# Four-bank token-major projections, branches ahead of retention, and an earlier start of the v product in a four-stage transformer on one core

## The chip, the cores and the metric

The program runs on one core of a Trainium2 chip. The time is what the device takes for one execution, in microseconds (us); runs of the same kernel are compared by their medians. All data lie in HBM at the start and the result is written back there. The core's engines are TensorE (PE in the rows, its weight loads PEld), VectorE (DVE), ScalarE (ACT), GpSimd (POOL) and SyncE (SP, which here only issues transfers).

## What is computed

The reference takes 512 tokens of width 1024 through these stages, all in float32:

- block 1: a norm, then two branches side by side, a gated delta rule in both directions and an attention with dilated windows, gated and added to the stream;
- a PEER layer: each token picks 16 of 16384 experts in each of 8 heads by two sets of 128 keys. An expert is one row of a table u and one of a table v: `y = sum over picked experts of weight * gelu(x . u_e) * v_e`;
- block 2, twice: a norm, then three branches of it, each with a gate of width 1024,

```
a = latent attention (MLA)      b = stick-breaking attention      c = retention
m = sigmoid(gate_a) * (a Wa) + sigmoid(gate_b) * (b Wb) + sigmoid(gate_c) * (c Wc)
h = h + m Wo
h = h + square(relu(norm(h) Wup)) Wdown
```

- the last row of the stream goes through a final norm.

## The kernel before

**Matmuls.** A float32 product is made of three matmuls on rounded halves: a number x is split into xh (rounded) and xl = x - xh, and W x becomes Wh xh + Wh xl + Wl xh. Weights come from HBM in tiles of 128x1024, 512 KB each, by SP's queue (`raw<-...`, method `pump`, line 632). ACT rounds such a tile to its high half and DVE subtracts to get the low half (both `whl<-raw` in the rows; `split`, `split_low`). Activations lie with features on partitions and 512 tokens along the columns, as eight tiles of 128x512 with a high and a low half (`s` in the rows). `unit` is the common product: one weight tile, 24 matmuls of 512 columns into one PSUM bank. The eight banks are two lists: `bmain` with two banks, for the products of the main path, and `bside` with six, for the side jobs (attention and so on).

**Order.** The program is written out instruction by instruction by the class `Prog`, in one order for each engine. The main path is a generator; after each piece of it a model of the clocks, kept while the program is built, decides whether a piece of a side job is put in between (`tick`), so that side work fills engines beside the main products. `wait` and `idle` let side work run on until a job is done. `BACKLOG`, `RAW` and `AHEAD` set how far side work and weights may run ahead. Each engine works its list in order; all helpers record through line 307, which is why nearly all rows have that line.

**Token-major projections.** Two of the branches need v with tokens on partitions. `tm_unit` (line 715) takes two weight tiles, which together hold 256 of 512 output columns for all 1024 inputs. It goes through four groups of 128 tokens, one after the other: 24 matmuls of 256 columns into one bank of `bmain`, then the bank is given to `tok_epi` (line 2046), which scales it on ACT into half a tile. Two calls, one for each half of the columns, make one projection: 192 matmuls, eight evictions. There are four projections: `stick` and `retain` in both layers.

**The peer stage** (`peer`). 384 tokens are computed densely: for each of 128 chunks of 128 experts, 24 matmuls of 384 columns against the tile of u (the u product), a gelu on ACT, and a write of the result to the DRAM tensor `ga` (the last 16 chunks are kept in SBUF). Side jobs route the tokens and write the experts' weights to the DRAM tensor `wd` (`wd<-big`, 24 writes on POOL's queue). The v product follows, with 128 chunks again, 24 matmuls each, and all eight banks accumulate through it (`acc`). For each chunk DVE multiplies gelu by the weights (`prep`, the `s<-s,big` rows), ACT and DVE split the product (`prep_low` makes the low half). `rows` reads the weights for eight chunks by three transfers of 512 KB (`big<-wd`). The first three of these, the first products and the job `rope_tables` (sines and cosines for block 2, a chain on DVE and ACT) are put in between u and v. The other 128 tokens are done by gathering single rows of u and v on POOL's queue (`picked`: `rows_u`, `rows_v`, products on DVE into `dbl`). The last two chunks (`last`) are kept back, so that the eight banks end one after the other, d = 0 to 7: for each, its last six matmuls and a transpose, then an addition on DVE, a scaled high half on ACT and a low half on DVE, which block 2 needs.

**Block 2** (`layer`). `ORDER` is: latents of branch a, 6 gate units, upward projections of a, projections of b (`stick`), 6 gate units, projections of c (`retain`), 12 gate units. A gate unit's result is written to the DRAM tensor `gd`. The side jobs of a, b and c run beside this. Then the main path waits for all three jobs, splits their 12 result tiles into halves (`hilo`), and makes the branches: for dp = 0 to 3 and each branch b two units of 12 matmuls, each multiplied by its sigmoid gate and summed. `Wo`, the norm and the MLP follow.

Of the kernel before, what the change touches and what calls it, by code (L numbers as in the profile page):

```python
# [26 lines left out]
TB = 16  # L27
# [48 lines left out]
BRANCHES = ((0, 0), (0, 2), (0, 4), (1, 0), (1, 2), (1, 4), (0, 6), (1, 6))  # L76
ORDER1 = ("da0", "k", "q", "da1", "da2", "v", "z", 16)
# [70 lines left out]
def layouts(x, norm_mix, w_in, dn_conv, dn_a_log, dn_dt_bias, dn_out_norm, rel_bias, w_branch_dn,  # L148
# [45 lines left out]
    for l in range(2):  # L194
# [21 lines left out]
        f[f"w_b{l}"] = np.stack([_fm_tiles(w_branch_2[l, b], 2) for b in range(3)], 1).reshape(12, 128, 1024)  # L216
# [94 lines left out]
class Prog:  # L311
# [403 lines left out]
    def tm_unit(self, xs, sels, epi):  # L715
        w0 = self.get()
        w1 = self.get(more=True)
        for n, sel in enumerate(sels):
            ps = self.bank(q=self.bmain)
            for i in range(8):  # L720
                hi, lo = (w0, w1)[i // 4]
                s = slice((i % 4) * 256, (i % 4) * 256 + 256)
                xh, xl = sel(xs[i][0]), sel(xs[i][1])
                m = xh.shape[1]
                self.mm(ps[:m, :256], xh, hi[:, s], start=i == 0, stop=False)
                self.mm(ps[:m, :256], xh, lo[:, s], start=False, stop=False)
                self.mm(ps[:m, :256], xl, hi[:, s], start=False, stop=i == 7)
                if i == 3:
                    self.flush()
            self.pend.append((lambda p, n=n, m=m: epi(n, p[:m, :256]), ps))  # L730
            yield
# [791 lines left out]
    def peer(self):  # L1523
# [43 lines left out]
        for c in range(128):  # L1567
            def epi(ps, c=c):
                t = self.slot(big=c < 128 - KEPT)
                self.act(t[:, :TD], ps[:, :TD], AF.Gelu_apprx_tanh)  # L1570
                if c < 128 - KEPT:
                    self.dma(ga[c], t[:, :TD], self.nc.sync)
                    self.put(t)
                else:
                    gts[c - 128 + KEPT] = t
            if c >= 128 - KEPT:
                self.room(4)
            yield from self.unit(self.get(), xs, epi)
        self.flush()
        self.wait(wt, rt_end)  # L1580
        self.put(ic)
        for a in self.xn:
            self.put(*a)
        self.BACKLOG, self.low_late = 4.0, True

        assert len(self.bmain) == 2 and len(self.bside) == 6
        acc = [self.bank(q=q) for q in (self.bmain, self.bside) for _ in range(len(q))]
        rt = self.add(self.rope_tables())
        self.close_big(1)
        bigs = [self.take_big(0), self.take_big(1)]  # L1590
        self.ring.extend(b[:, 8 * TD:8 * TD + 1024] for b in bigs)

        def rows(n, t0, k):
            w = bigs[n % 2][:, :8 * TD].rearrange("p (t i u) -> p t i u", i=8, u=TB)
# [27 lines left out]

        def step(d, c, v, h):
# [6 lines left out]
        for i in range(3):  # L1630
            rows(0, i * 8, 8)
        for c in range(6):
            fetch(c)
        for c in range(3):
            prep(c)
        prep_low(0)
        prep_low(1)
        last = range(126, 128)
        for c in range(last[0]):
            fetch(c + 6)  # L1640
            if c % 8 < 3 and c < 120:
                rows(c // 8 + 1, c % 8 * 8, 8)
# [960 lines left out]
```

## Time and profile before

| | |
|---|---|
| median of 3 runs | 3900.13 us (3897.69 to 3905.33) |
| the profiled execution | 3899.97 us, span 3898.0 us |
| TensorE busy | 3772.4 us, 97% of the span |
| mean granted TensorE clock | 0.986 |
| VectorE, ScalarE, GpSimd busy | 2541.1 (65%), 1536.9 (39%), 457.6 us (12%) |
| moved by transfers | 666.67 MB, mean 171 GB/s |

The span is the time from the first to the last instruction of one core; the execution's own time has some 2 us around it. Busy time of TensorE is the time in which a matmul is under way, at whatever clock; the granted clock is a share of full speed. A number in square brackets behind a row is the time for which the engine stood idle just before it, with what ended this.

### The profile page before, as it was taken

How to read it: one execution, taken by the hardware profiler on the slowest of the kernel's cores; microseconds unless marked ns; L12 is line 12 of the kernel's file. 1: busy time of each engine (PE TensorE's matmuls, PEld its weight loads, DVE VectorE, ACT ScalarE, POOL GpSimd, SP SyncE). 2: the span in 40 equal slices, each digit the busy share in tenths (PEclk: the TensorE clock that was granted, in tenths of full speed). 3: DMA queues.
4: the chain of work that ended last, by engine and by line, in shares of the span. 5: the costliest groups of instructions: out<-in, count | busy, mean ns of one | idle time of the engine just before them, and what ended most of it. 6: DMA issues, size and time to landing. Idle time of an engine off the chain costs nothing.

```text
span 3898.0 us, 56154 instructions
## 1 busy us (share of the span) xinstructions
PE 3772.4 (97%) x21866; PEld 3221.4 (83%) x21866; DVE 2541.1 (65%) x4608; ACT 1536.9 (39%) x2392; POOL 457.6 (12%) x524
## 2 busy tenths in 40 slices
PE   9999899999999979999989999999999999999998
PEld 6777777899889979999977876788888878678886
DVE  4565755789989868888766556654345656564334
ACT  3533334344545423333343453433233344343222
POOL 1010201011333433222200001000000001000000
PEclk9999999999999989999999999999999999999999
DMA  4232524376798989999933223432233223342222
GB/s 151 81 110 88 168 101 151 129 240 209 291 329 296 380 285 326 348 345 348 342 123 108 76 78 120 154 119 97 96 106 128 87 77 100 109 167 105 95 95 81
DMA packets 259114, 666.67 MB, mean 171 GB/s; under 512 B 27316, under 2 KB 105428, under 8 KB 255776
## 3 DMA queue, kind: packets, MB, share of 16 engines
q1 hardware_dynamic: 202752, 457.19, 34.3%
q0 software_dynamic: 55376, 204.80, 14.5%
q8 instruction: 172, 2.82, 0.3%
q10 hardware_dynamic: 720, 1.08, 0.1%
q14 instruction: 94, 0.77, 0.1%
HBM read 576.16 MB, written 81.57 MB: 169 GB/s over the span
## 4 chain that ended last, share of the span: by engine, by line
PE 58%; DVE 2%; ACT 2%; issue 1%; DMA 0%; DVEq 0%; ACTq 0%
PE bank L307 58%; DVE s L307 1%; ACT s L307 1%; DVE big L307 1%; ACT whl L307 0%; DMA big<-rope 0%; DVE whl L307 0%; ACT L555 0%; ACT big L307 0%; DVE mla_m L307 0%; DVE dbl L307 0%; ACT dbl L307 0%; DVE bank L307 0%; DVEq L2598 0%; DVEq L307 0%
## 5 line engine op out<-in xcount | busy, mean ns | idle before, releaser
L307 PE MATMUL bank<-s,whl 128*128 128x512 f32 (+1 forms) x15156 | 3276.1, 374 | 89.3 <-DVE whl L307 28.7
L307 PEld LDWEIGHTS bank<-s,whl 128*128 128x128 f32 x15156 | 2756.9, 189 | 502.4 <-issue 66.7
L307 DVE TENSOR_TENSOR whl<-raw,whl 128x1024 fp32r<-128x1024 f32 x651 | 795.1, 1222 | 484.1 <-ACT whl L307 481.0
L307 ACT ACTIVATE whl<-raw 128x1024 fp32r<-128x1024 f32 x651 | 683.1, 1055 | 685.3 <-PE bank L307 368.5
L307 DVE TENSOR_TENSOR big<-bank,big 128x512 f32<-128x512 f32 (+4 forms) x270 | 179.0, 666 | 300.0 <-PE bank L307 297.1
L307 DVE TENSOR_TENSOR s<-s,s 128x1024 f16<-128x1024 f16 (+9 forms) x498 | 295.1, 614 | 23.2 <-ACT s L307 13.2
L307 ACT ACTIVATE s<-bank 128x384 f32<-128x384 f32 (+6 forms) x263 | 122.0, 489 | 414.1 <-PE bank L307 406.6
L307 ACT ACTIVATE big<-big 128x512 f32<-128x512 f32 (+2 forms) x235 | 141.6, 615 | 323.4 <-DVE big L307 277.7
L307 ACT ACTIVATE big<-bank 128x512 f32<-128x512 f32 (+3 forms) x242 | 161.2, 712 | 254.5 <-PE bank L307 157.5
L307 ACT ACTIVATE s<-s 128x384 fp32r<-128x384 f32 (+7 forms) x321 | 162.6, 526 | 155.2 <-DVE s L307 151.1
L307 PE MATMUL bank<-s,s 128*128 128x128 f16 (+10 forms) x2102 | 209.2, 260 | 4.6 <-DVE s L307 4.6
L1701 POOL DMA_INDIRECT dbl<-rows_u,s x128 | 172.1, 1345 | 321.8 <-DVE dbl L307 135.3
L307 DVE TENSOR_TENSOR s<-s,big 128x384 f32<-128x384 f32 (+5 forms) x279 | 135.1, 488 | 47.1 <-DMA big<-wd 20.3
L582 POOL DMA_DIRECT2D s<-dbl x16 | 7.9, 500 | 1319.6 <-PE bank L307 1319.6
L307 DVE SCALAR_TENSOR_TENSOR dbl<-dbl,dbl 128x1024 f32<-128x1024 f32 x128 | 154.3, 1217 | 10.0 <-DMA dbl<-rows_u,s 10.0
L307 PEld LDWEIGHTS bank<-s,s 32*32 32x32 f32 (+5 forms) x1334 | 104.4, 146 | 37.0 <-issue 26.2
L1701 POOL DMA_INDIRECT dbl<-rows_v,s x94 | 103.6, 1102 | 258.9 <-DVE dbl L307 252.4
L307 ACT ACTIVATE s<-big 128x512 fp32r<-128x512 f32 (+2 forms) x136 | 90.6, 677 | 106.7 <-DVE big L307 104.7
L307 PE MATMUL bank<-s,big 32*32 32x32 f32 (+6 forms) x960 | 121.2, 283 | 1.7 <-ACT big L307 1.3
L307 PE MATMUL bank<-whl,s 128*128 128x256 f32 (+1 forms) x816 | 111.7, 297 | 9.3 <-ACT s L307 6.0
L307 DVE SCALAR_TENSOR_TENSOR dbl<-dbl,s,dbl 128x1024 f32<-128x1024 f32 x93 | 118.8, 1278 | 0.0
L307 DVE SCALAR_TENSOR_TENSOR big<-bank,big 128x512 f32<-128x512 f32 x74 | 51.0, 690 | 103.0 <-PE bank L307 98.9
(260 smaller groups left out, 2135.5 us busy)
## 6 DMA issues: line engine op xcount, KB each, us to landing
raw<-u SPq DMA_DIRECT2D x128, 512.0 KB, 5.4
raw<-v SPq DMA_DIRECT2D x128, 512.0 KB, 6.8
raw<-w_mlp SPq DMA_DIRECT2D x128, 512.0 KB, 3.4
wd<-big POOLq DMA_DIRECT2D x24, 1024.0 KB, 7.7
big<-wd SPq DMA_DIRECT2D x48, 512.0 KB, 10.1
raw<-w_g SPq DMA_DIRECT2D x48, 512.0 KB, 3.5
s<-ga SPq DMA_DIRECT2D x112, 192.0 KB, 7.4
raw<-w_da SPq DMA_DIRECT2D x36, 512.0 KB, 3.5
```

Of the source, the lines that this page charges most:

```text
L307: return getattr(self.eng, f)(*a, **k)
L582: (eng or self.queue).dma_start(out, in_)
L1701: self.nc.gpsimd.indirect_dma_start(buf, None, self.I[table], bass.IndirectOffsetOnAxis(ap=idx, axis=0))
```

## The change

It has three parts. First, `tm_unit` opens four banks at once (two of `bmain`, two of `bside`), takes one weight tile after the other, each with two blocks of 128 inputs for all 512 columns, and goes through the four groups of tokens within each block. The matmuls have 512 columns, 96 for a projection, and the four banks are evicted at the end. Second, in block 2 the branches a and b are made for all dp before retention's, with the weight tiles in that order, the 12 result tiles are split by side jobs (`split_parts`) that run from the last 12 gate units on, and the gates are fetched one at a time. Third, in the peer stage the first reads of `wd` go out during u, three chunks after the last write of it is recorded, and the first three chunks of v are prepared beside the chunks 124 to 127 of u; `rope_tables` is added at v's ninth chunk; three chunks are kept for the end of v in place of two; from chunk 116 on two raw weight tiles are read ahead in place of four.

```diff
 def _tm_tiles(w):
     k, n = w.shape
-    t = w.reshape(2, 4, 128, n // 256, 256).transpose(3, 0, 2, 1, 4)
-    return np.ascontiguousarray(t.reshape(n // 256 * 2, 128, 1024))
+    t = w.reshape(4, 2, 128, n).transpose(0, 2, 1, 3)
+    return np.ascontiguousarray(t.reshape(4, 128, 1024))
...
+BRANCHES2 = (*((b, dp) for dp in range(4) for b in range(2)), *((2, dp) for dp in range(4)))
...
-    def tm_unit(self, xs, sels, epi):
...
+    def tm_unit(self, xs, epi):
+
+        self.flush()
+        ps = [self.bank(q=q) for q in (self.bmain, self.bside, self.bside, self.bmain)]
+        for i in range(8):
+            if i % 2 == 0:
+                hi, lo = self.get()
+            s = slice(i % 2 * 512, i % 2 * 512 + 512)
+            xh, xl = xs[i]
+            for n in range(4):
+                c = slice(n * 128, n * 128 + 128)
+                self.mm(ps[n], xh[:, c], hi[:, s], start=i == 0, stop=False)
+                self.mm(ps[n], xl[:, c], hi[:, s], start=False, stop=False)
+                self.mm(ps[n], xh[:, c], lo[:, s], start=False, stop=i == 7)
+                if i == 7:
+                    epi(n, ps[n])
+                    self.unbank(ps[n])
+                if n % 2:
+                    yield
...
+        came = None
         for c in range(128):
...
             yield from self.unit(self.get(), xs, epi)
+            if came is None and wt.done:
+                came = c
+            if came is not None:
+                if came + 3 <= c < came + 6:
+                    rows(0, (c - came - 3) * 8, 8)
+
+                if came + 6 <= 124 <= c:
+                    {124: prep, 125: prep, 126: prep, 127: prep_low}[c](min(c - 124, 2) if c < 127 else 0)
+                    if c == 127:
+                        prep_low(1)
...
-        acc = [self.bank(q=q) for q in (self.bmain, self.bside) for _ in range(len(q))]
-        rt = self.add(self.rope_tables())
+        acc = sorted([self.bank(q=q) for q in (self.bmain, self.bside) for _ in range(len(q))],
+                     key=lambda a: self.read.get(self.key(a), 0))
...
-        for i in range(3):
-            rows(0, i * 8, 8)
-        for c in range(6):
-            fetch(c)
-        for c in range(3):
-            prep(c)
-        prep_low(0)
-        prep_low(1)
-        last = range(126, 128)
...
+        last = range(125, 128)
         for c in range(last[0]):
...
+            if c == 8:
+                rt = self.add(self.rope_tables())
             if c == 116:
+                self.RAW = 2
...
         def tok_epi(lst):
...
+            def epi(n, ps):
+                lst.append(self.slot())
+                self.act(lst[n], ps, scale=res["col"][:, n:n + 1])
+            return epi
...
-            for half in range(2):
-                yield from self.tm_unit(xs, NAT, tok_epi(v)(half))
-            self.flush()
+            while len(self.bside) < 2:
+                self.idle()
+            yield from self.tm_unit(xs, tok_epi(v))
...
+        parts, splits = [[], [], []], {}
         for p in ORDER:
+            for b, y in enumerate((ya, yb, yc)):
+                if b not in splits and "abc"[b] in job and isinstance(p, int) and p == ORDER[-1]:
+                    splits[b] = self.add(self.split_parts(job["abc"[b]], y, parts[b]))
...
-        self.wait(*(job[x] for x in "abc"))
-        ys = [[self.hilo(t) for t in y] for y in (ya, yb, yc)]
...
+        for b, dp in BRANCHES2:
+            if len(ys) <= b:
+                if b == 2:
+                    self.flush()
+                self.wait(splits[b])
+                ys.append(parts[b])
...
+            w = self.get()
+            for j in range(2):
+                fetch()
...
+                yield from self.unit(w, ys[b], epi, o=j * 512)
```

The `last` chunks, the branches' epilogue (gate times product, sum, late split) and the code that is not shown stay as they were, but for names. All helpers' line is 309 after the change.

How the change moves instructions stands below at three places. The first is DVE's list where u ends and v begins, before (names: `big_74` holds the rows of wd; `whl` is a low half of a weight tile; `dbl` belongs to the picked tokens):

```order
L307 TENSOR_TENSOR whl<-raw,whl 128x1024
L307 SCALAR_TENSOR_TENSOR dbl_5970<-dbl_5974,s_6112,dbl_5970 128x1024
L307 TENSOR_TENSOR s_12669<-s_12669,big_74 128x384
L307 TENSOR_TENSOR s_12708<-s_12708,big_74 128x384
L307 TENSOR_TENSOR s_12742<-s_12742,big_74 128x384
L307 TENSOR_TENSOR s_13194<-s_12669,s_13186 128x384
L307 TENSOR_TENSOR s_13196<-s_12708,s_13189 128x384
L307 TENSOR_TENSOR s_13202<-s_12742,s_13192 128x384
L307 TENSOR_TENSOR s_12776<-s_12776,big_74 128x384
L307 SCALAR_TENSOR_TENSOR dbl_5970<-dbl_5975,s_6112,dbl_5970 128x1024
L307 CAST s_13219<-s_13217 128x512
```

The same place with the change:

```order
L309 TENSOR_TENSOR s_12672<-s_12672,big_74 128x384
L309 TENSOR_TENSOR whl<-raw,whl 128x1024
L309 SCALAR_TENSOR_TENSOR dbl_5970<-dbl_5972,s_6112,dbl_5970 128x1024
L309 TENSOR_TENSOR s_12711<-s_12711,big_74 128x384
L309 TENSOR_TENSOR whl<-raw,whl 128x1024
L309 SCALAR_TENSOR_TENSOR dbl_5970<-dbl_5973,s_6112,dbl_5970 128x1024
L309 TENSOR_TENSOR s_12745<-s_12745,big_74 128x384
L309 SCALAR_TENSOR_TENSOR dbl_5970<-dbl_5974,s_6112,dbl_5970 128x1024
L309 TENSOR_TENSOR whl<-raw,whl 128x1024
L309 TENSOR_TENSOR s_13192<-s_12672,s_13082 128x384
L309 TENSOR_TENSOR s_13194<-s_12711,s_13119 128x384
```

The three products with the rows of wd stood in a row behind u's last weights; now each stands between two chunks of u, and the CAST that opens the rope tables is gone from here. The second place is DVE's list inside v with the change, where the first block of the rope tables begins and the second begins at the end of the piece:

```order
L309 CAST s_13519<-s_13517 128x512
L309 TENSOR_SCALAR s_13522<-s_13519,in_c_base 128x512
L309 TENSOR_SCALAR s_13523<-s_13522 128x512
L309 TENSOR_SCALAR s_13523<-s_13523 128x512 x2
L309 SCALAR_TENSOR_TENSOR s_13524<-s_13523,s_13522 128x512
L309 SCALAR_TENSOR_TENSOR s_13524<-s_13523,s_13524 128x512 x2
L309 TENSOR_SCALAR s_13524<-s_13524 128x512 x2
L309 TENSOR_TENSOR s_13560<-s_13065,s_13512 128x384
L309 TENSOR_TENSOR s_13099<-s_13099,big_75 128x384
L309 TENSOR_TENSOR whl<-raw,whl 128x1024
...
L309 TENSOR_TENSOR whl<-raw,whl 128x1024
L309 SCALAR_TENSOR_TENSOR dbl_5970<-dbl_5971,s_6112,dbl_5970 128x1024
L309 TENSOR_SCALAR s_13523<-s_13522 128x512
```

A block stands undivided between the operations of two chunks, and two chunks lie between the beginnings of two blocks. The third place is TensorE's list at the first token-major projection, before (`bank_76` and `bank_77` are the main banks):

```order
L307 MATMUL bank_77<-whl,s_18197 128x256 x2
L307 MATMUL bank_77<-whl,s_18198 128x256
L307 MATMUL bank_77<-whl,s_18212 128x256 x2
L307 MATMUL bank_77<-whl,s_18213 128x256
L307 MATMUL bank_77<-whl,s_18224 128x256 x2
```

The same place with the change:

```order
L309 MATMUL bank_77<-whl,s_18172 128x512
L309 MATMUL bank_77<-whl,s_18173 128x512
L309 MATMUL bank_77<-whl,s_18172 128x512
L309 MATMUL bank_82<-whl,s_18172 128x512
L309 MATMUL bank_82<-whl,s_18173 128x512
L309 MATMUL bank_82<-whl,s_18172 128x512
L309 MATMUL bank_81<-in_c_base,s_19480 128x128 x4
L309 MATMUL bank_80<-in_c_base,s_19481 128x128 x4
L309 MATMUL bank_83<-whl,s_18172 128x512
```

One bank stayed the target through all eight input blocks; now the target changes from bank to bank within one block.

## Rows read from the trace of the kernel before

**Rows 1.** The page: span, and TensorE's busy time, share and instructions.
```profile
span 3898.0 us, 56154 instructions
...
PE 3772.4 (97%) x21866; PEld 3221.4 (83%) x21866; DVE 2541.1 (65%) x4608; ACT 1536.9 (39%) x2392; POOL 457.6 (12%) x524
```

**Rows 2.** Windows: length, busy us (instructions) of PE, PEld, DVE, ACT, POOL; clock; DMA share, GB/s.
```profile
1600.00:1700.00 100.00, 100.00 (x578) 100.00 (x578) 80.87 (x98) 35.34 (x48) 24.17 (x24) 1.00 0.99 350
1432.00:1475.00 43.00, 33.75 (x157) 32.07 (x158) 41.80 (x66) 16.12 (x22) 13.36 (x11) 0.87 0.55 176
```

**Rows 3.** Timeline at v's start: start us, us, engine, line, operation, count [idle before].
```profile
1416.00 7.87 SPq L582 DMA_DIRECT2D big<-wd  x4
1430.87 1.50 DVE L307 TENSOR_TENSOR s<-s,big 128x384 f32<-128x384 f32 x3 [15.52 <-DMA big<-wd]
1432.04 0.69 PE L307 MATMUL bank<-s,whl 128*128 128x384 f32 x1 [12.29 <-ACT s L307]
```

**Rows 4.** Lines by form, DVE, 1435 to 1464: busy us, mean ns, idle before.
```profile
L307 DVE SCALAR_TENSOR_TENSOR s<-s,s 128x512 f32<-128x512 f32 x12 | 8.3, 692 | 0.6
L307 DVE TENSOR_SCALAR s<-s 128x512 f32<-128x512 f32 x18 | 7.7, 426 | 0.5
```

**Rows 5.** Timeline of the v product, DVE and PE, 1902 to 1960.
```profile
1902.60 1.23 DVE L307 TENSOR_TENSOR whl<-raw,whl 128x1024 fp32r<-128x1024 f32 x1 [0.80 <-ACT whl L307]
...
1935.27 0.56 DVE L307 TENSOR_TENSOR s<-s,big 128x384 f32<-128x384 f32 x1 [4.82 <-DMA big<-wd]
...
1923.79 36.39 PE L307 MATMUL bank<-s,whl 128*128 128x384 f32 x209
```

**Rows 6.** Late in u: PE's wait, a window, SP's timeline, and the tile wd.
```profile
1330.90 11.37 PE L307 MATMUL bank<-s,whl 128*128 128x384 f32 x55 [4.06 <-DVE whl L307]
...
1320.00:1330.00 10.00, 6.84 (x40) 6.52 (x38) 5.22 (x9) 2.87 (x4) 2.82 (x4) 1.00 1.03 402
...
1318.72 0.33 SPq L582 DMA_DIRECT2D ga<-big  x1
...
L582 POOL DMA_DIRECT2D wd<-big x24: 576/576/582, 931.1 to 1310.1; - x24
```

**Rows 7.** Timeline of v's end: first and eighth addition on DVE, then PE's next matmul.
```profile
1973.33 0.69 DVE L307 TENSOR_TENSOR s<-bank,s 128x512 f32<-128x512 f32 x1 [2.94 <-PE bank L307]
...
1988.34 0.68 DVE L307 TENSOR_TENSOR s<-bank,s 128x512 f32<-128x512 f32 x1
...
1991.75 2.50 PE L307 MATMUL bank<-s,whl 128*128 128x512 f32 x5 [9.78 <-DVE whl L307]
```

**Rows 8.** Timeline of PE in a projection; a window of block 2 with 512 columns.
```profile
2308.01 8.90 PE L307 MATMUL bank<-whl,s 128*128 128x256 f32 x72
...
2600.00:2800.00 200.00, 200.00 (x882) 165.11 (x881) 83.31 (x96) 64.46 (x81) 0.00 (x0) 1.00 0.29 98
```

**Rows 9.** Timeline of PE and ACT in layer 0's projections, and a window there.
```profile
2157.70 2.53 PE L307 MATMUL bank<-whl,s 128*128 128x256 f32 x19 [1.64 <-DVE s L307]
...
2311.56 0.93 ACT L307 ACTIVATE s<-s 128x384 f32<-128x384 f32 x2
...
2319.91 5.36 PE L307 MATMUL bank<-whl,s 128*128 128x256 f32 x30 [3.00 <-ACT s L307]
...
2319.00:2330.00 11.00, 10.09 (x71) 10.09 (x72) 10.30 (x20) 5.09 (x11) 0.00 (x0) 0.84 0.13 48
```

**Rows 10.** Timeline of PE before the branches of layer 0, and a window there.
```profile
2473.86 0.50 PE L307 MATMUL bank<-s,whl 128*128 128x512 f32 x1 [1.96 <-ACT s L307]
2475.46 7.74 PE L307 MATMUL bank<-s,whl 128*128 128x512 f32 x21 [1.09 <-DVE s L307]
...
2473.00:2483.00 10.00, 8.05 (x22) 6.17 (x23) 8.69 (x15) 9.97 (x18) 0.00 (x0) 0.66 0.99 332
```

**Rows 11.** Waits of PE from 1992 to the end: us in total, times, longest.
```profile
PE bank L307 <- ACT s L307: 10.9, 6, 3.0
...
PE bank L307 <- DVE s L307: 5.9, 6, 1.6
```

More of the change, by code (lines that the diff above doesn't have):

```diff
@@ L215, in layouts @@
         f[f"w_u{l}"] = u
-        f[f"w_b{l}"] = np.stack([_fm_tiles(w_branch_2[l, b], 2) for b in range(3)], 1).reshape(12, 128, 1024)
+        br = [_fm_tiles(w_branch_2[l, b], 2) for b in range(3)]
+        f[f"w_b{l}"] = np.stack([br[b][dp] for b, dp in BRANCHES2])
         f[f"w_o{l}"] = _fm_tiles(w_out_2[l], 1)
@@ L1566, in peer @@
         gts, wts, his, hs = {}, {}, {}, {}
[L1567 to L1586, printed above, removed]
-        acc = [self.bank(q=q) for q in (self.bmain, self.bside) for _ in range(len(q))]
-        rt = self.add(self.rope_tables())
-        self.close_big(1)
-        bigs = [self.take_big(0), self.take_big(1)]
-        self.ring.extend(b[:, 8 * TD:8 * TD + 1024] for b in bigs)
         def rows(n, t0, k):
-            w = bigs[n % 2][:, :8 * TD].rearrange("p (t i u) -> p t i u", i=8, u=TB)
+            w = self.big[n % 2][:, :8 * TD].rearrange("p (t i u) -> p t i u", i=8, u=TB)
             c = V_ORDER[8 * n]
@@ L1621, in prep_low, with epi @@
                 hs[c] = hi, lo
+        came = None
+        for c in range(128):
+            def epi(ps, c=c):
+                t = self.slot(big=c < 128 - KEPT)
+                self.act(t[:, :TD], ps[:, :TD], AF.Gelu_apprx_tanh)
+                if c < 128 - KEPT:
+                    self.dma(ga[c], t[:, :TD], self.nc.sync)
+                    self.put(t)
+                else:
+                    gts[c - 128 + KEPT] = t
+            if c >= 128 - KEPT:
+                self.room(4)
+            yield from self.unit(self.get(), xs, epi)
+            if came is None and wt.done:
[8 more added lines that the diff above has]
+        self.flush()
+        self.wait(wt, rt_end)
+        self.put(ic)
+        for a in self.xn:
+            self.put(*a)
+        self.BACKLOG, self.low_late = 4.0, True
+        assert len(self.bmain) == 2 and len(self.bside) == 6
+        acc = sorted([self.bank(q=q) for q in (self.bmain, self.bside) for _ in range(len(q))],
+                     key=lambda a: self.read.get(self.key(a), 0))
+        self.close_big(1)
+        bigs = [self.take_big(0), self.take_big(1)]
+        self.ring.extend(b[:, 8 * TD:8 * TD + 1024] for b in bigs)
         def step(d, c, v, h):
@@ L2134, in retain @@
             self.room(self.ROOM + 2)
-            for half in range(2):
-                yield from self.tm_unit(xs, NAT, tok_epi(v)(half))
-            self.flush()
+            while len(self.bside) < 2:
+                self.idle()
+            yield from self.tm_unit(xs, tok_epi(v))
             t1 = self.add(self.rope_large(q, ()))
@@ L2251, in layer, with split_parts @@
         self.st = st2
+    def split_parts(self, t, src, dst):
+        yield from self.until(t)
+        for x in src:
+            yield from self.need(slots=3)
+            dst.append(self.hilo(x))
+            yield
     def latent(self, cq, ck, gq, gk, lat, res):
```

85 lines of the change are left out of this document (34 added, 51 removed).

## The prediction

> **What bounds the kernel now.** I read the page first: TensorE is busy for 97% of the span [rows 1], so time can only be won where it waits, where its clock falls, or by giving it fewer or cheaper matmuls. The profiled execution took 3899.97 us against the median of 3900.13 us of the runs, so a sum made against it stands for the median; a measurement of this kernel tells about 0.2%, 7.8 us, from no change. Next come the windows: in the middle of the v product TensorE is busy without a gap at full clock, 578 matmuls in 100 us, 173.0 ns each; around the start of v it is not, with 157 matmuls in 43 us and a granted clock of 0.87 [rows 2]. The timeline of that stretch shows why [rows 3]. TensorE has finished u at 1432.04 - 12.29 = 1419.75 and waits 12.29 us. ACT, which the row names, itself waited for DVE, and DVE waited 15.52 us for the transfers of wd that SP issued only at 1416.00. Third, TensorE's own waits from the end of the peer stage to the end of the program: some 32 us in all, the longest the 9.78 us at the end of v [rows 7], and twelve short ones on small tiles of ACT and DVE [rows 11].
>
> **Part 1, v's start.** Before, it loses 12.29 us of waiting, and then 43.0 - 157 x 0.173 = 15.8 us by gaps and clock [rows 2, 3], 28.1 in all. The second piece comes from DVE, which makes there, besides the weights' low halves, the rope tables: 12 operations of 8.3 us and 18 of 7.7 us [rows 4], with three smaller pieces of some 0.45 us (estimate) 17.4 us. After the change the three reads of wd go out while u runs, and the products and the high and low halves of the first chunks are spread between u's last operations (first order fence). I take the whole 28.1 as saved, less 0.5 for the switch itself.
>
> The rope tables are then due from v's ninth chunk on, in four blocks two chunks apart (second order fence); at 692 and 426 ns an operation [rows 4] the blocks take about 5.1, 3.8, 4.7 and 3.8 us. In steady v DVE has 0.80 us free in each chunk of 24 x 0.173 = 4.15 us [rows 2, 5], so two chunks take in 1.6 us of each block, and 17.4 - 4 x 1.6 = 11.0 us pile up. Against that stands a lead. At 1935.27 DVE had stood 4.82 us for a transfer, and TensorE went through it in one row of 209 matmuls without a wait [rows 5]. So the lead is at least 4.8 us. By the code a chunk's high half is made two chunks before its use, 8.3 us, less 1.23 us for DVE's low half [rows 5] and some 1.1 for ACT's high half (estimate: no longer than the low one), which leaves about 6.0. So 11.0 - 6.0 = 5.0 us of waits are left, in the third and fourth block. After a wait of 3.00 us the granted clock was 0.84 over 11 us, which cost 0.16 x 10.09 = 1.6 us [rows 9]; I add 1.7. The cost is 6.7 us, between 0 (the lead is larger) and 17.4 + 4 x 1.7 = 24.2 (no cover at all).
>
> The moved reads cost something in u. Three reads of 512 KB come into a stretch where DMA is full: from 1320 to 1330 its share is 1.03 at 402 GB/s, and TensorE works 6.84 of these 10 us, because DVE, in order, stands behind late gathers; the wait ends at 1330.90 and is 4.06 us [rows 6]. 1.5 MB at 402 GB/s are 3.9 us of transfers. If gathers come later by all of it TensorE pays that and a stretch at lower clock, some 5.7; if the load has passed by then, 0. By order the three reads stand on SP behind the `ga` writes of chunks 104 to 106, the first of which went out at 1318.72 [rows 6], so they fall into this very stretch; the last write of wd starts at 1310.1 and lands after at most 16.1 us, so the first read may hold SP until 1326, and the next weights with it, of which four chunks are ahead. I take 4.0, nearer to the upper end. **The Trainium skill**, "DMA: Bandwidth & Descriptors", section "Issuing engines are not separate DMA queues", says that transfers started by sync and by GpSimd run on the same 16 engines and interleave. The row of 1.03 agrees, and by that rule SP's reads do delay POOL's gathers: the whole 5.7 would then stand in the sum.
>
> v's start and its price: 28.1 - 0.5 - 6.7 - 4.0 = **16.9 us**.
>
> **Part 2, v's end.** The eight additions that close v run as a chain on DVE and ACT, from 1973.33 to 1988.34 for seven steps, 2.144 us each; TensorE's own work per step is shorter, so it ends early and waits 9.78 us [rows 7]. With three chunks kept for the tail in place of two, 24 matmuls more (4.2 us) lie beside that chain, which starts 3 x 0.173 = 0.5 us later in it. Gain 3.6; at least 2, since the last products of the picked tokens come two chunks nearer to the tail. I take **3.5**.
>
> **Part 3, the token-major projections.** Before, one is 192 matmuls of 256 columns, 8.90 us for 72, or 123.6 ns each; a matmul of 512 columns takes 200 us / 882 = 226.8 ns [rows 8]. So 192 x 0.1236 = 23.7 becomes 96 x 0.2268 = 21.8, 2.0 us each, **7.8** in four. The Trainium skill, "TensorE: Matmul & The Clock Gate", section "Back-to-back issue gap", gives an isolated gap of columns / 2.4 + 2.5 ns; by it 192 x 109.2 and 96 x 215.8 ns differ by only 0.24 us, 1.0 for all four. Both rows are longer than that formula, the short shape by more, so the rows decide.
>
> Before, the two main banks must be evicted one by one in the middle of the projection, and TensorE waits 1.64 us in the first (on DVE, for a bank of the unit before) and 3.00 us in the second (on ACT), with 1.6 us of clock behind it [rows 9]. The eviction at the second stands behind ACT's side work that had begun by 2311.56. Layer 1 has the same: the two waits tables count six each, with totals of about twice one layer's [rows 11]. That is 2 x (1.64 + 3.00 + 1.6) = 12.5 us. With four banks nothing is evicted within a projection (third order fence). At its end four evictions of 512 columns follow each other on ACT, while the next unit needs only the first bank, ready three banks' last matmuls (9 x 0.227 = 2.0 us) before. I keep 2 us for that: **10.5**.
>
> **Part 4, the branches.** Before, all three jobs must end, and then ACT and DVE split 12 tiles while TensorE has nothing: 1.96 and 1.09 us of waiting, and 8.05 us of work at a clock of 0.66, which costs 0.34 x 8.05 = 2.7 [rows 10]. In layer 1 the clock may cost nothing or the same; I take 1.3. That is 2 x 3.05 + 4.0 = 10.1. After, the splits lie beside the last gates, and retention comes last. By order it now ends four units into the branches; the two other branches have 16 units of 12 matmuls, so 12 x 12 x 0.227 = 33 us lie between its end and its first product. I keep 1: **9.1**. More table loads on ACT (four per layer) lie beside matmuls.
>
> **Sum.** 16.9 + 3.5 + 7.8 + 10.5 + 9.1 = 47.8. Waits that nobody sees yet (fewer side banks in the projections, gates fetched one by one) I put at 3. 3900 - 45 gives **3855 us**.
>
> **The rivals.**
> - Rope blocks unhidden: DVE's lead is used up by something else (the gathers' products stand in the same queue), the four blocks stop TensorE by their whole length and its clock falls: 24.2 in place of 6.7, 3872 us. Chance 0.13. For it: in the stretch from 1435 just this work stopped TensorE four times. Against it: those chunks had no lead left.
> - Columns bring nothing: a matmul's time goes by its columns alone, 192 x 113.4 = 96 x 226.8 ns, and nothing is saved: 3863 us. The 123.6 ns of [rows 8] speak against it; 0.04. The Trainium skill's formula, in part 3, comes to about this.
> - Transfers: the moved reads cost all of 5.7 or, with SP standing long and the weights behind it late, some 10 us: 3857 to 3861 us. For it: the share of 1.03; against it: four chunks of weights ahead. 0.10.
> - All covers hold: no rope waits, no new waits, no price in u: 45 + 6.7 + 3 + 4 = 58.7, 3841 us. For it: the lead of DVE is only bounded from below; 0.15.
> - Not what it says: the reads of wd go out early only if all writes are recorded by a certain chunk. By order they do, so that the old place stays in use is excluded but for a stop of SP.
> - Slower: the four evictions in a row stand behind a burst of ACT's side work, the next unit waits for the main bank. The burst seen ran from 2311.56 to the wait's end at 2319.91 [rows 9], 8.4 us; with 1.6 us of clock that is 10.0 at each of four ends, 40 us in place of the 2 that I kept: 3893. It becomes slower than before from some 11.7 us at each end (47 / 4), and by more than 0.2% from 13.7: then 3908 us. Against it: the table shows no wait on ACT over 3.0 us [rows 11]. 0.03.
>
> **How the numbers follow.** The forecast has 0.53, rope 0.13, columns 0.04, transfers 0.10, all covers 0.15, slower 0.03, and 0.02 for the same burst at a price that ends within 0.2%. The range goes from 3838 (all covers, and 3 us of the gains that I took low) to 3875 (rope unhidden, and 3 us more), which leaves out under 2 in 10. Faster by over 0.2% 0.95, within 0.2% 0.02, slower 0.03.
>
> **What would show it.** Right: no wait of TensorE over 1 us between u and v; 100 us windows of v at clock 1.00 but for one near the rope blocks, with DVE busy there; a wait at v's end near 6 us; 96 rows of 128x512 in a projection at 227 ns with no wait inside; no wait before the branches and clock 1.00 over them. Wrong: waits on `whl` through 40 us behind v's ninth chunk (rope); a longer gap near 1330 (transfers); waits of the unit after a projection on ACT; and the same 28 us at v's start if wd arrives late there after all.

## The result, and the profile after

The changed kernel takes 3857.2 us (median of 4 runs, 3855.68 to 3859.36), the kernel before in runs beside it 3898.91 us: a ratio of 0.989, 95% interval 0.9874 to 0.9906, or 42 us less. The page of the changed kernel, its span and the row of busy time [rows 1]:

```profile
span 3855.7 us, 55396 instructions
...
PE 3756.0 (97%) x21482; PEld 3189.1 (83%) x21482; DVE 2540.1 (66%) x4608; ACT 1547.5 (40%) x2384; POOL 463.4 (12%) x524
```

384 matmuls are gone (4 x 96), and the share of TensorE is the same: it still sets the time. To see where the time went, the span is cut in three by two rows that every kernel here has: A ends where a row of 110 matmuls late in u begins, B where TensorE resumes after v's tail, C with the span. Up to the end of A no kernel of this study differs from another in TensorE's list.

| profiled execution | A | B | C |
|---|---|---|---|
| before | 1307.5 | 684.2 | 1906.3 |
| changed | 1305.3 | 659.0 | 1891.4 |
| difference | -2.2 | -25.2 | -14.9 |

A alone scatters from 1304.5 to 1310.6 over the kernels of this study, so a median that moves by 3 us says little here, and B and C say more. C scatters too: four kernels whose TensorE works the same list in C (changed, runs 4, 8 and 12) have a C of 1888.5 to 1893.9. In these four TensorE's idle time in C is nearly the same, 30.1 to 30.8 us, while the time in which the lower of the clock's two levels (1.2 and 2.4 GHz) was granted goes from 14.6 to 26.8 us. So below some 5 us it is the idle time that tells, not C. The PE timeline of the changed kernel from late in u into v, and its first products after v's tail:

```profile
1305.34 19.32 PE L309 MATMUL bank<-s,whl 128*128 128x384 f32 x110
1327.84 47.63 PE L309 MATMUL bank<-s,whl 128*128 128x384 f32 x264 [3.17 <-DVE whl L309]
1376.19 91.82 PE L309 MATMUL bank<-s,whl 128*128 128x384 f32 x528 [0.72 <-DVE whl L309]
1468.90 8.25 PE L309 MATMUL bank<-s,whl 128*128 128x384 f32 x46 [0.89 <-DVE whl L309]
1478.66 0.62 PE L309 MATMUL bank<-s,whl 128*128 128x384 f32 x2 [1.51 <-ACT whl L309]
1480.32 8.27 PE L309 MATMUL bank<-s,whl 128*128 128x384 f32 x46 [1.04 <-DVE whl L309]
1489.09 0.62 PE L309 MATMUL bank<-s,whl 128*128 128x384 f32 x2 [0.51 <-ACT whl L309]
1490.75 455.03 PE L309 MATMUL bank<-s,whl 128*128 128x384 f32 x2623 [1.04 <-DVE whl L309]
...
1959.62 0.78 PE L309 MATMUL bank<-s,whl 128*128 128x512 f32 x2 [1.86 <-DVE s L309]
1964.35 17.59 PE L309 MATMUL bank<-s,whl 128*128 128x512 f32 x64 [3.95 <-DVE whl L309]
```

The wait of 12.29 us at v's start [rows 3] is gone: one row of 528 matmuls runs across it. Five waits of 4.99 us together stand behind the second to fourth block of rope tables; the window of 1450 to 1500 shows TensorE busy for 45.02 us at clock 1.00, so there they cost no clock. At the end of v 1.86 + 3.95 = 5.81 us stand for 9.78 [rows 7].

In block 2 the waits inside the projections [rows 9] are gone, and others have come. First the unit after which TensorE waits in layer 0, with ACT and DVE ahead of it (timeline of the changed kernel):

```profile
2240.99 0.93 ACT L309 ACTIVATE big<-big 128x384 f32<-128x384 f32 x2
...
2245.71 1.33 ACT L309 ACTIVATE s<-s,in_c_base 128x512 f32<-128x512 f32 x2
2246.94 1.04 ACT L309 ACTIVATE whl<-raw 128x1024 fp32r<-128x1024 f32 x1
2248.02 1.22 DVE L309 TENSOR_TENSOR whl<-raw,whl 128x1024 fp32r<-128x1024 f32 x1 [7.56 <-ACT whl L309]
2249.16 0.68 DVE L309 TENSOR_TENSOR s<-bank,big 128x512 f32<-128x512 f32 x1
2249.90 5.97 PE L309 MATMUL bank<-s,whl 128*128 128x512 f32 x18 [2.71 <-DVE s L309]
```

A weight's high half stands behind 6 us of activations of the stick-breaking job, DVE stands 7.56 us for it, and behind DVE's low half stands the eviction that frees TensorE's bank. The second new wait is at the first branch (same timeline, SP, ACT and PE):

```profile
2425.14 8.64 SPq L584 DMA_DIRECT2D gate<-s  x2
2433.83 0.42 SPq L584 DMA_DIRECT2D big<-gate  x1
2436.54 0.63 ACT L309 ACTIVATE big<-big 128x512 f32<-128x512 f32 x1 [14.04 <-DMA big<-gate]
2438.94 0.58 ACT L309 ACTIVATE dbl<-bank 128x512 f32<-128x512 f32 x1
2439.57 0.70 PE L309 MATMUL bank<-dbl,big 128*128 128x512 f32 x1 [2.67 <-ACT dbl L309]
```

SP holds the first gate read behind the write of the last gate unit, which has yet to end; ACT waits 14.04 us for that read with the first sigmoid, and an eviction of the retention job, on which TensorE waits, is queued behind this sigmoid, a second one and a weight. The waits table of the changed kernel from 1965 to the end [rows 11]:

```profile
PE bank L309 <- DVE s L309: 8.0, 4, 2.7
PE bank L309 <- ACT dbl L309: 5.2, 2, 2.7
...
PE bank L309 <- ACT s L309: 0.7, 2, 0.3
```

The windows of C, before and changed (length, then TensorE's busy time):

```profile
1991.75:3898.00 1906.25, 1870.71 (x8978) 1491.54 (x8978) 1038.91 (x1653) 727.15 (x1193) 31.31 (x64) 0.99 0.31 106
1964.35:3855.70 1891.35, 1861.20 (x8594) 1465.80 (x8594) 1039.24 (x1653) 738.04 (x1185) 31.43 (x64) 0.99 0.31 107
```

### The profile page after: what moved, and what is told of

Read it like the earlier page. It is cut to its first block, busy times and chain, and to the rows that moved or that the text cites. A ratio compares the mean times of both kernels' runs of the same rounds, so it can differ in the third digit from the quotient of the medians.

```text
span 3855.7 us, 55396 instructions
## 1 busy us (share of the span) xinstructions
PE 3756.0 (97%) x21482; PEld 3189.1 (83%) x21482; DVE 2540.1 (66%) x4608; ACT 1547.5 (40%) x2384; POOL 463.4 (12%) x524
## 4 chain that ended last, share of the span: by engine, by line
PE 70%; DVE 4%; DMA 3%; ACT 2%; issue 2%; POOL 1%; SPq 0%; DVEq 0%; ACTq 0%; POOLq 0%
PE bank L309 70%; DMA ga<-big 3%; DVE s L309 2%; DVE whl L309 1%; DVE big L309 1%; ACT big L309 1%; ACT s L309 1%; ACT whl L309 1%; POOL dbl L1721 1%; DVE dbl L309 0%; DMA dbl<-rows_u,s 0%; DMA s<-gate 0%; DVE ix L309 0%; DVE mla_m L309 0%; DMA raw<-u 0%
## 5 line engine op out<-in xcount | busy, mean ns | idle before, releaser
L309 DVE TENSOR_TENSOR s<-s,s 128x1024 f16<-128x1024 f16 (+8 forms) x478 | 286.0, 618 | 24.1 <-ACT s L309 13.8
L309 ACT ACTIVATE big<-bank 128x512 f32<-128x512 f32 (+4 forms) x254 | 166.7, 701 | 280.5 <-PE bank L309 185.6
L309 ACT ACTIVATE s<-bank 128x384 f32<-128x384 f32 (+5 forms) x251 | 117.1, 488 | 361.8 <-PE bank L309 354.9
L309 ACT ACTIVATE s<-s 128x384 fp32r<-128x384 f32 (+7 forms) x289 | 149.2, 529 | 174.0 <-DVE s L309 168.9
L309 PE MATMUL bank<-s,s 128*128 128x128 f16 (+9 forms) x1988 | 194.6, 254 | 4.0 <-DVE s L309 4.0
L584 POOL DMA_DIRECT2D s<-s x24 | 11.9, 504 | 1289.9 <-PE bank L309 1289.2
L309 ACT ACTIVATE s<-big 128x512 fp32r<-128x512 f32 (+3 forms) x146 | 95.3, 662 | 64.9 <-DVE big L309 62.9
L309 PEld LDWEIGHTS bank<-s,s 32*32 32x32 f32 (+5 forms) x1220 | 94.2, 143 | 30.0 <-issue 20.6
L309 PE MATMUL bank<-whl,s 128*128 128x512 f32 x432 | 110.3, 403 | 0.0
L309 PE MATMUL bank<-s,big 32*32 32x32 f32 (+8 forms) x916 | 105.8, 284 | 1.6 <-ACT big L309 1.2
```

Source lines behind the costliest of these rows:

```text
L309: return getattr(self.eng, f)(*a, **k)
L584: (eng or self.queue).dma_start(out, in_)
```

## The experiments

The three parts were first run alone on the kernel before, then parts of the changed kernel were undone or mended. Stretches in the text are A, B and C as above.

**1. The projections alone.** The kernel before with the new `_tm_tiles`, `tm_unit` and `tok_epi`:

```diff
-            for half in range(2):
-                yield from self.tm_unit(xs, NAT, tok_epi(v)(half))
-            self.flush()
+            while len(self.bside) < 2:
+                self.idle()
+            yield from self.tm_unit(xs, tok_epi(v))
```

> The kernel before with only the projections of the change (four banks, 512 columns). Theory A (the wait moved): the columns save 7.8 us in four projections and the waits inside them go (2 x 4.64 us and 2 x 1.6 us of clock, 12.5), but the burst of activations of the stick-breaking job on ACT, which made the longer of them, now stops an ordinary product once in each layer, 2.7 us and some 1 us of clock: 7.8 + 12.5 - 7.4 = 13 us less than before, about 3886 us; a wait of 2 to 3 us on DVE or ACT stands in each layer within 60 us of the second projection, and none inside a projection. Theory B (as predicted): nothing takes the place of the waits, 18 us less, about 3881 us. Theory C (a matmul's time goes by its columns alone): the spacing at 512 columns inside the projection is twice that at 256, and at most 9 us are saved, 3890 us or more.

Measured: 3914.64 us, ratio 1.0047 (1.003 to 1.0064): slower than before. C is 1922.6, 16 us more than before, and all three theories fail on the time. The waits of 2.71 us that theory A named are there, two in each layer and not one. The PE timeline of this kernel shows where the retention job ends, and two windows there:

```profile
2450.34 1.64 PE L307 MATMUL bank<-s,whl 128*128 128x512 f32 x6
...
2456.81 0.95 PE L307 MATMUL bank<-dbl,s 64*128 64x128 f32 x4 [3.34 <-DVE big L307]
...
2474.50 1.13 PE L307 MATMUL bank<-big,big 128*128 128x512 f32 x2 [1.44 <-ACT big L307]
2477.59 0.50 PE L307 MATMUL bank<-s,whl 128*128 128x512 f32 x1 [1.96 <-ACT s L307]
...
2400.00:2500.00 100.00, 90.55 (x389) 56.84 (x388) 52.34 (x86) 32.45 (x51) 0.00 (x0) 0.95 0.39 128
2450.00:2480.00 30.00, 20.55 (x77) 9.17 (x74) 14.67 (x28) 7.96 (x14) 0.00 (x0) 0.87 0.30 97
```

The last product of the main path ends at 2452, and for 25 us TensorE has only the retention job's own short chain, with waits and a lower clock. Before, main path and job ended together [rows 10]. The job is also late by itself. By form and count of the rows its first products stand here, before and in this run:

```profile
2404.66 1.13 PE L307 MATMUL bank<-dbl,s 64*128 64x512 f32 x4
...
2412.39 1.13 PE L307 MATMUL bank<-s,big 64*128 64x512 f32 x4
```

From the beginning of C that is 412.9 and 426.1 us. In both kernels the last sums of the stick-breaking job end some 5 us ahead of them, so the delay is already in this job; why it is later beside the new projections was not tried.

**2. The peer stage alone** (all of the change in `peer`, nothing else).

> The kernel before with only the change in the peer stage (early reads of wd and first products, later rope tables, three chunks kept for the tail). Theory A: by the two traces v's start gives 21.6 us (28.1 of before less 5.0 of waits at the rope tables and some 1.5 of clock in u) and the tail 3.7: 25 us less than before, about 3874 us. Theory B (as predicted, with 1.7 of clock and 4.0 in u): 20.4 us, about 3879 us. Theory C: a part of the gain at v was only a difference between two executions, 2.2 us of which stood already ahead of the changed place: 23 us, 3876 us.

Measured: 3873.67 us, ratio 0.9936 (0.992 to 0.9953), 21.7 us less; B 657.7, C 1907.0 as before. Four kernels with the peer stage of before (before, runs 1, 3 and 5) have a B of 681.1 to 684.2 (mean 682.1), five with the changed one (changed, runs 2, 6, 7 and 11) 657.7 to 659.4 (mean 658.7): the part gives 23.4 us by B, between theories A and C, and 21.7 by the medians, between B and C. Only the sizes differ between the theories, by less than the scatter, so none is singled out.

**3. The branches alone** (`BRANCHES2`, `split_parts`, gates fetched one by one).

> The kernel before with only the change of the branches (splits by side jobs, retention last, gates fetched one at a time). Theory A (the gain was given back): the waits of 1.96 and 1.09 us and some 4 us of clock go, 10 us in both layers, but SP stands before the gate reads behind the last gates' writes, ACT stands behind the first sigmoid, and TensorE waits 2.6 us on an eviction in the retention job and 1.3 us before the output product, 7.8 in both layers: 2 us less than before, within 3895 to 3898 us. Theory B (as predicted): 9 us less, 3890 us, and no wait of TensorE over 1 us between the last gates and the output product.

Measured: 3898.87 us beside 3895.37, ratio 1.0005 (0.9996 to 1.0015): nothing gained. That is theory A in kind, though the 2 us that it left did not come. The wait on ACT in the retention job is larger than expected (PE timeline of this kernel):

```profile
2472.20 2.08 PE L309 MATMUL bank<-big,big 128*128 128x512 f32 x2 [4.22 <-ACT big L309]
```

So one part costs 16 us of C, one 4, and both together save 15. They belong together: with the projections alone the retention job ends after the main path, and the branches put other main work beside its end.

**4. The rope tables spread.**

```diff
         for f in range(2):
             self.ts(ang, pos, self.freq[:, f:f + 1])
+            yield 1.7
...
                 self.ts(n, ang, 1.0 / two_pi, sh, OP.mult, OP.add)
+                yield 1.7
```

and so behind each of the DVE operations.

> The changed kernel with the rope tables made one DVE operation per chunk of v over 33 chunks, in place of four blocks two chunks apart. Theory A (DVE's room per chunk and its lead set the cost): one operation of 0.43 to 0.69 us fits in the 0.80 us that each chunk leaves free, so the five waits behind 1468 us, 5.0 us in all, go: about 3852 us, v without a wait over 0.2 us. Theory B (the waits there come from the transfers of that stretch or the picked tokens' products): waits of the same size stay, 3857 us.

Measured: 3852.04 us, ratio 0.9885 (0.9869 to 0.9902); B 652.5. Theory A: the PE timeline shows v in one row.

```profile
1378.43 563.17 PE L309 MATMUL bank<-s,whl 128*128 128x384 f32 x3247 [0.70 <-DVE whl L309]
```

**5. The projections with more cover.** The first kernel, with

```diff
-ORDER = ("c", 6, "u", "sb", 6, "r", 12)
+ORDER = ("c", 6, "u", "sb", "r", 18)
```

> The kernel of the first run (only the projections changed, 3914.6 us) with all 18 remaining gate units behind retention's projections, in place of 6 ahead and 12 behind: the same work, six units of 24 matmuls (33 us) more beside the retention job. Theory A (that run lost because the retention job ends after the last gate unit, with about 24 us in each layer in which TensorE has nothing but this job): the job ends beside the gates, the waits of 3.3, 1.1 and 1.4 us there go and the clock stays up, 25 to 30 us less than that run, 3885 to 3890 us. Theory B (four banks and 512 columns are themselves slower, by held side banks): the time stays over 3905 us, and the retention job ends as late against its own start.

Measured: 3876.41 us, ratio 0.9949 (0.9932 to 0.9966): 38 us less than the first kernel with the same work, and C is 1885.3, 21 us less than before. Theory A, and more than it gave: the four waits of 2.71 us of the first run, which it did not count, are gone too. So four banks and 512 columns do not make block 2 slower in every order. What they gain is not shown, since the kernel before was not run with this order of gates alone, and part of the 21 us may come from the order. The retention job's end before the branches leaves one wait (PE timeline):

```profile
2466.53 13.67 PE L307 MATMUL bank<-s,whl 128*128 128x512 f32 x59 [1.16 <-DVE s L307]
```

**6. Gates read early.** In `gates`, with `fetch` moved ahead of it and no first fetch behind:

```diff
                 yield from self.unit(self.get(), xs, epi)
+                if b == 20:
+                    self.room(6)
+                    for _ in range(3):
+                        fetch()
```

> The changed kernel with the first three gate reads issued three gate units earlier, ahead of the last gates' writes on SP. Theory A (SP, in order, holds the reads behind writes that wait for the last gate unit; ACT stands behind the first sigmoid, and TensorE on ACT): ACT's idle time of 14 us before that sigmoid and TensorE's waits of 2.7 and 2.5 us on an eviction go, 5 us less, about 3852 us. Theory B (the retention job's own chain sets the wait): a wait of about the same length stays on DVE or ACT, 3857 us.

Measured: 3856.19 us (3851.46 to 3859.96), ratio 0.9888 (0.9872 to 0.9905). The median tells nothing, since A was 5.3 us longer in the profiled execution. C is 1887.9, 3.5 us less, which is within the scatter of C, but the waits table of C has no row for ACT `dbl` any more (5.2 us in the changed kernel), and TensorE's idle time in C is 25.0 us for 30.2. Theory A.

**7. The stick-breaking job's activations in two steps.**

```diff
                 self.act(wn[e], wn[e], AF.Exp)
+            yield
             for e in range(2):
                 self.act(wn[e], wn[e], AF.Ln, bias=self.one)
```

> The changed kernel with the stick-breaking job's exponentials and logarithms given to ACT in two steps in place of one. Theory A (a burst of some 6 us of its activations stands ahead of a weight's high half, DVE behind that, and TensorE 2.7 us behind an eviction on DVE): the burst is cut, the two waits of 2.7 us and some 1.5 us of clock behind each go, 6 to 8 us less, about 3850 us. Theory B (the order shifts, and another burst takes its place): a wait of 2 to 3 us appears elsewhere in the same job, 3857 us.

Measured: 3853.81 us, ratio 0.9888 (0.9871 to 0.9904); C 1884.0, 7.3 us less. The waits of 2.71 us are gone, and so are those at the first sigmoid, which this edit does not touch: the order shifted. New ones of 1.4 to 1.5 us came, two in each layer (PE timeline; then a row of the waits table of C):

```profile
2346.35 4.37 PE L309 MATMUL bank<-s,whl 128*128 128x512 f32 x18 [1.53 <-DVE s L309]
...
PE bank L309 <- DVE s L309: 8.4, 6, 1.5
```

This row was 8.0 us in the changed kernel: cutting the burst split the waits and did not lessen them, which is theory B, though no new wait is as long as 2 us. The idle time of C fell from 30.2 to 25.0 us, as much as the waits at the first sigmoid had been, and the rest of the 7.3 us is clock. So theory A has the size by luck; why the waits at the sigmoid went is open.

**8. Two chunks in the tail.**

```diff
-        last = range(125, 128)
+        last = range(126, 128)
```

> The changed kernel with two chunks of v kept for the tail, as before, in place of three. Theory A (24 matmuls beside a chain of eight steps of 2.14 us): TensorE's waits at the end of v add up to 9.5 us again in place of 5.8, 3.7 us more, about 3861 us. Theory B (the chain itself starts later by the picked tokens' last products, so that the third chunk gains nothing): 3857 us.

Measured: 3867.41 us, ratio 0.9925 (0.9909 to 0.9942). PE timeline at the end of v:

```profile
1965.16 1.19 PE L309 MATMUL bank<-s,whl 128*128 128x512 f32 x2 [5.52 <-DVE s L309]
1969.89 16.97 PE L309 MATMUL bank<-s,whl 128*128 128x512 f32 x64 [3.54 <-DVE whl L309]
```

9.06 us for 5.81: 3.25 more, theory A. The medians differ by 10 us; of the rest 2.6 each stand in A and in C, where nothing was changed. In C the idle time is that of the changed kernel (30.4 and 30.2 us) and the lower clock was granted for 26.8 us in place of 20.8.

**9. The three edits together** (4, 6 and 7).

> The changed kernel with the three edits of the earlier runs together: rope tables one operation per chunk, gates read early, the stick-breaking job's activations in two steps. Theory A (three separate waits): by the traces 5.0, 3.5 and 7.3 us less, 15.8 in all, about 3841 us; by the medians of the three runs 5.2, 1.0 and 3.4, 9.6 in all, 3848 us; between these. Theory B (one order feeds the next, so that a wait removed comes back elsewhere): 3852 us or more, with new waits of TensorE over 1.5 us in block 2.

Measured: 3845.89 us (3842.85 to 3851.44), ratio 0.9869 (0.9852 to 0.9885), the fastest kernel of the study: 52 us less than before and 11 less than the changed kernel, between the two sums of theory A. C is 1884.6, no better than in run 7 alone: the edits 6 and 7 removed the same wait, so the three waits were not separate, and the edit of the gates adds nothing here.

**10. The same with all 18 gate units behind the projections** (`ORDER` as in run 5).

> The run before with all 18 remaining gate units behind retention's projections. Theory A (the branches of a and b already cover the retention job): within 4 us of the run before. Theory B (the retention job still stops TensorE): 5 to 10 us less than the run before, waits in the retention job gone.

Measured: 3868.32 us, ratio 0.9928 (0.9911 to 0.9944), 22 us slower than run 9; both theories fail. PE timeline and a window of this kernel before the branches:

```profile
2427.56 7.07 PE L309 MATMUL bank<-s,whl 128*128 128x512 f32 x30
2437.48 0.50 PE L309 MATMUL bank<-s,s 128*128 128x512 f32 x1 [2.85 <-ACT s L309]
...
2447.77 0.50 PE L309 MATMUL bank<-s,whl 128*128 128x512 f32 x1 [1.21 <-ACT s L309]
...
2400.00:2500.00 100.00, 92.53 (x404) 74.28 (x403) 62.99 (x96) 52.54 (x82) 0.00 (x0) 0.97 0.44 147
```

Main work ends at 2434.6, and for 13 us a job runs alone again. By the form of its rows (sums of 128x512 from `s`) it is the stick-breaking job, which the order of branches needs before retention; that this is what became late was read from the forms, not tried.

**11. Cover by gates in place of the branches' part.** Projections, peer stage and `ORDER` as in run 5, with the branches of before.

> The projections' and the peer stage's part without the branches' part, but with all 18 remaining gate units behind retention's projections. Theory A (the branches' part is worth what it covers of the retention job, and gates cover it as well): 3876.4 less the 21.7 us of the peer stage, 3855 us, the same as the changed kernel. Theory B (the splits by side jobs and the order of branches gain by themselves): 9 us more than the changed kernel, 3866 us.

Measured: 3858.21 us, ratio 0.9901 (0.9884 to 0.9917), the same as the changed kernel within the scatter; C 1885.2, 6 us less than with the branches' part. Theory A: with this order of gates the branches' part is not needed, and run 10, which has both, is slower (3868.32 us).

**12. The first reads of wd late again.** The rope tables stay at v's ninth chunk:

```diff
-            if came is None and wt.done:
-                came = c
```

> The changed kernel with the first reads of wd and the first products put between u and v again, the rope tables staying at v's ninth chunk. Theory A (of the 28.1 us at v's start, 12.3 are the wait for wd and 15.8 come from the rope tables on DVE): 12.3 us of wait and some 3 us of clock come back, 15 us more than the changed kernel, 3872 us, with no wait over 1 us in the five chunks behind it. Theory B (the second piece comes from the late start, since DVE has no lead then): also waits of 2 to 3 us in these chunks come back, 22 to 28 us more, 3880 us or more.

Measured: 3874.62 us, ratio 0.9946 (0.9929 to 0.9962), 17 us more; B is 672.6, 13.5 us more. PE timeline at v's start:

```profile
1424.01 0.69 PE L309 MATMUL bank<-s,whl 128*128 128x384 f32 x1 [9.81 <-ACT s L309]
1424.86 42.88 PE L309 MATMUL bank<-s,whl 128*128 128x384 f32 x239 [0.16 <-DVE s L309]
1470.05 0.61 PE L309 MATMUL bank<-s,whl 128*128 128x384 f32 x2 [2.31 <-ACT whl L309]
```

The wait is back, and behind it come 239 matmuls without a stop, where before four waits of 1.35 to 2.81 us stood. So the second piece of the loss at v's start was the rope tables on DVE: theory A.

## Why the prediction was right

The time, 3857.2 us, lies 2 us above the 3855 forecast and in the range of 3838 to 3875; it is faster by more than 0.2%. That it came so near is in part luck: in the profiled executions the peer stage gave 4.8 us more than was forecast and A, where nothing changed, 2.2, while block 2 gave 9.5 less, and there the terms were wrong one by one.

**Part 1** forecast 16.9 us with its prices. The 28.1 us split in kind as it said: in run 12 the wait is back, at 9.81 us, and the losses behind it are not. The rope tables' waits were put at 5.0 us, from DVE's room of 0.80 us per chunk and a lead of 6.0 us; they are 4.99, one of them (0.89) already behind the second block, and run 4 removes them by that same room. The 1.7 of clock did not come there (1.00 in the window). The price in u was put at 4.0: late in u the waits are 3.17 + 0.72 = 3.89 us, against 2.29, 2.33, 2.61, 3.55 and 4.06 in five kernels without early reads, so about 1 us. The rival that would add 5.7 us there names the right place, but the added transfers cost little. The Trainium skill's rule on shared engines behind it ("DMA: Bandwidth & Descriptors", "Issuing engines are not separate DMA queues") says that transfers interleave, and not what this costs. **Part 2** forecast a gain of 3.5 us and a wait near 6: it is 5.81, and run 8 gives 3.25 back. B together saved 25.2 us in these two executions, and 23.4 by the means of run 2, where 20.4 were forecast.

**Parts 3 and 4** were forecast at 7.8 + 10.5 + 9.1, less 3 for new waits, 24.4 us; C gave 14.9. In the forecast 7.8 us are columns, 15.4 are waits that go, less 6 (2, 1 and 3) kept for others, and 7.2 are clock. By the windows of C TensorE's idle time fell by 5.4 us, from 35.5 to 30.2, and its busy time by 9.5. The lower clock level was granted for 35.7 us of C before and 20.8 after, and TensorE was busy in 21.4 and 9.4 of them; at half the clock this makes 6.0 of the 9.5, about as much as the clock scatters between executions of the same list. 3.5 us are left for the matmuls themselves. So two steps failed.

The first is the columns term. The prediction divided 8.90 us by 72 matmuls, but this time runs to the end of the last one, and a matmul lasts longer than the distance to the next. The rows by form give the mean length as their last number before the idle time, before and changed, in ns, and the PE timeline the 24 matmuls of a projection in the changed kernel:

```profile
L307 PE MATMUL bank<-whl,s 128*128 128x256 f32 x72 | 8.9, 284 | 0.0
...
L309 PE MATMUL bank<-whl,s 128*128 128x512 f32 x24 | 5.7, 394 | 0.0
...
2270.89 5.71 PE L309 MATMUL bank<-whl,s 128*128 128x512 f32 x24
```

From start to start that is (8.90 - 0.28) / 71 = 121.4 ns for 256 columns and (5.71 - 0.394) / 23 = 231.1 ns for 512. So 192 x 0.1214 = 23.3 us became 96 x 0.2311 = 22.2, 1.1 us each and 4.4 in four, where 7.8 were forecast. In runs 5 and 11, with the same columns but another order of the gates, TensorE's busy time in C less this half of the lower clock is 1860.1 and 1859.9 us, and 1860.0 in the kernel before. So even these 4.4 are not shown to reach the time. By the formula of the Trainium skill ("TensorE: Matmul & The Clock Gate", "Back-to-back issue gap") the columns term would be 1.0 us, an estimate. Both shapes are longer than that formula, by 12 and 15 ns, and not the short one by more, as the prediction has it.

The second is the 6 us kept for waits. 2.71, 2.67 and 1.28 us stand in layer 0 and as much in layer 1, 13 us in both. The prediction had put gates fetched one by one and fewer side banks among its 3 us for what nobody sees yet; the order of SP and ACT at the first gate alone costs 5.2 (run 6). The 2.71 stand behind a burst on ACT of the kind that stopped an eviction of the projection before; now it stops one of the products ahead of the projection (run 7 splits these waits but does not lessen them). In the slower rival it is likewise a burst on ACT that decides, but behind the four evictions; those made no wait. Of the signs named for block 2, no wait inside a projection and clock 1.00 over the branches came, and no wait before the branches did not (2.67).

What the prediction did not say is that its terms hold only together. By runs 1 and 3 the projections alone cost 16 us, and the branches alone gain nothing. The cover that part 4 counted, 33 us, is there: behind the retention job's last matmul in the changed kernel one row of 262 matmuls runs to the wait in front of the output product. Less the 96 of retention's own branch these are 166, or 38 us.

```profile
2453.86 60.00 PE L309 MATMUL bank<-s,whl 128*128 128x512 f32 x262
2515.14 1.21 PE L309 MATMUL bank<-s,whl 128*128 128x512 f32 x4 [1.28 <-DVE s L309]
```

Without it the job ends 25 us after the main path (run 1). The 21 us that C saves in runs 5 and 11 do not confirm part 3's two terms, 18.3 us, near as they are: there the waits of part 4 on ACT, 1.96 us in each layer, are gone too, and the order of the gates is another.

## What to carry to other kernels

A change to the bottleneck's own work can leave the end of a chain that ran beside it without cover: before adding up its gain, ask which side job ends last, how much later than the main work it will then end, and what stands behind it. Parts that give each other cover are priced together, not one by one. When a wait is removed from one in-order queue, follow the burst that made it to the next instruction queued behind it. Take the time of a row of overlapping instructions from start to start, without the last one's length. And put reads that something early needs ahead of writes that must wait, on the same queue.

## What the runs showed that was not expected

A chain with no other product beside it runs TensorE at a lower clock as well as with waits: 0.87 from 2450 to 2480 in run 1, where the retention job stands alone for 25 us, and 1.00 in the changed kernel from 2400 to 2500. And the same matmuls up to late in u took from 1304.5 to 1310.6 us in the fourteen profiled executions, and the same ones in C from 1888.5 to 1893.9 with nearly the same idle time. So under 5 us neither a median nor the length of a stretch settles a question; the waits in it do.
